# Ada rows two ahead, fetches behind the softening, and the opening's ada sums in two halves of the array

## The chip, the cores and the metric

The kernel runs on one core of a Trainium2 chip. The metric is the device time of one execution in microseconds, the median over several runs. Names of engines: PE or TensorE does matmuls (PEld is its weight load), ACT or ScalarE activations and casts, DVE or VectorE elementwise work, POOL or GpSimd small helpers, SP or SyncE issues most DMAs.

## The reference

Two layers of a diffusion transformer on 256 latent tokens `x` and 256 context tokens `ctx`, width 1024, all in fp32. Layer 0 mixes by retention, layer 1 by neighbourhood attention; each has an MLP with a hidden width of 4096.

```python
for i in range(DEPTH):
    mod = (silu_c @ ada_w[i] + ada_b[i])[:, None, :]      # ada_w[i]: 1024 x 6144
    mod_c = silu_cc @ ada_w[i] + ada_b[i]
    sh1, sc1, g1, sh2, sc2, g2 = jnp.split(mod, 6, axis=-1)
    ...
    h = x * (1.0 + sc1) + sh1
    hc = ctx * (1.0 + sc1c) + sh1c
    y, yc = retention_mixer(...) if i % 2 == 0 else neighbourhood_mixer(...)
    x = layer_norm(DN_ALPHA * x + g1 * y, ln_g[i, 0], ln_b[i, 0])
    h = x * (1.0 + sc2) + sh2
    x = layer_norm(DN_ALPHA * x + g2 * sq_relu_mlp(h, mlp_w1[i], mlp_w2[i]), ln_g[i, 1], ln_b[i, 1])
    # layer 0 does the same for ctx
```

The neighbourhood attention adds a bias to scores of 32 heads and takes a softmax over 512 local and 256 context columns. The ada products (one row per kind of token times a 1024 x 6144 matrix) give shift, scale and gate of every layer.

## The kernel before, in words

**Products.** Every fp32 product is made of three fp32r products: an operand is split into `hi` (a cast on ACT) and `lo` (a subtraction on DVE), and hi·hi, lo·hi and hi·lo are summed in PSUM. Weights come in units of 512 KB: `fetch` asks SP for a `raw` tile and casts it, `lows` subtracts, `take` hands units to the matmuls. The `raw` tiles come from a pool of four buffers, `rawp`, and the ada rows of the background (`rawa`) come from the same four. SP issues loads in the order of the program, and a load waits until its buffer is let go.

**Queues.** `pe.on`, `act.on`, `dve.on` and `sp.on` say where an engine keeps the order in which the code is written. Where they are off, a scheduler orders the instructions; in the middle of the layer-0 MLP it does.

**Background.** The ada products after the first chunks are not done on PE. `bg_stream` weighs one ada row tile per step on DVE (`weigh`, tile `acc` or `spare`), keeping one load ahead. After eight steps a part is complete; `folded` sums it into `red`, and a closure goes into `due`: `ada_columns` or `ada_gate`, a small matmul (`pada<-red,cst` in the trace) with DVE and DMA work behind it. The next call of `bg` runs what is in `due` and then the next step. In the layer-0 MLP `bg` is called once after each weight unit of the second product. A unit there is 24 matmuls: four token tiles (`mm2`), two row blocks, three products. `bg_max` is 31 before the MLP of layer 0 and 87 in it. The gate of the MLP, `G2`, is read back from DRAM (`grow`) by `load_gate`, in two broadcasts of 512 KB.

**MLP, second product.** Two halves of 512 output columns, each with four PSUM banks `p2` and eight units; after a half `accumulate` multiplies each bank by the gate on DVE (`acc<-p,G`). There are eight PSUM banks in all. The trace cuts numbers off names, so `p1` and `p2` are both `p` there.

**Opening.** Eight chunks of 128 columns of the model width. For each chunk `chunk_sums` makes the ada sums for shift and scale on PE: 16 matmuls with 32 output rows, dealt to four column groups of the array (`pada<-rawq,cT`); `chunk_row` copies the sums to SBUF; `chunk_columns` turns them into columns with two matmuls (`pada<-cst,row`), `chunk_turn` transposes the tokens (`pt<-cst,R`, `pada<-cst,R`), `chunk_modulate` makes `hTh` and `hTl`, and `chunk_q` and `part_v` project. Between them stand the parts of the chunk before.

**Attention of layer 1.** A list `STEPS` gives, for each group of heads, how many units to fetch and split before the softening (`early`), after it (`late`) and after the inversion (`last`), and which projections to run. A step sends 12 score matmuls (`pqk`), softens (four reductions on DVE, four exponentials on ACT), runs a projection, and turns the probabilities of the step before (`ppt`, copied to `pt` by ACT and DVE, `flip`).

```python
gather(n + 1); turned(n)
fetch(early); lows(early)
scores(n + 2); soften(n + 2)
fetch(late); lows(late)
run(before); flip(n + 1); invert(n + 2); fetch(last); attend(n); run(after)
lows(100 if n < len(STEPS) - 2 else len(STEPS) - 1 - n)
```

Of the kernel before, what the change touches and what calls it, by code (L numbers as in the profile page):

```python
# [17 lines left out]
P = 128  # L18
# [86 lines left out]
def kernel(  # L105
# [50 lines left out]
    def bank(s="ps"):  # L156
        return psp.tile([P, 512], F32, tag="ps", name=nm(s))
# [279 lines left out]
    def ada_columns(l, w, red, c0, nt):  # L437

        pr = bank("pada")
        for j in range(4):  # L440
            pe.matmul(
                pr[32 * j : 32 * j + 32, 0 : 8 * nt],
                lhsT=cv("fold"),
                rhs=red[:, :nt].rearrange("p t (k j) -> p j (t k)", j=4)[:, j],
                start=True,
                stop=True,
                tile_position=(0, 32 * j),
            )
        dve.tensor_add(
            out=mods[l, w][:, :, c0 : c0 + 4, :],  # L450
            in0=(
                pr[:, 0:16].rearrange("p (t s k) -> p s k t", t=2, s=2)
                if nt == 2
                else pr[:, 0:8].rearrange("p (s k) -> p s k", s=2).unsqueeze(3).broadcast_to([P, 2, 4, 2])
            ),
            in1=acol[:, COLUMNS.index((l, w)), :, c0 : c0 + 4].unsqueeze(3).broadcast_to([P, 2, 4, 2]),
        )

    def ada_gate(l, w, red, nt):

        tmp = scr("gate")[0:32, :]
        bias, tot, row = tmp[:, 0:32], tmp[:, 64 : 64 + 32 * nt], tmp[:, 128 : 128 + 32 * nt]
        g = (3 * w + 2) * D
        pool.dma_start(out=bias, in_=ada_b[l][g : g + D].rearrange("(b i) -> b i", i=32))
        pr = bank("pada")
        pe.matmul(
            pr[0:32, 0 : 32 * nt], lhsT=cv("fold"), rhs=red[:, :nt].rearrange("p t b -> p (t b)"),
            start=True, stop=True, tile_position=(0, 0),
        )
        dve.transpose(out=tot, in_=pr[0:32, 0 : 32 * nt])  # L470
        dve.tensor_add(
            out=row.rearrange("p (t i) -> p t i", t=nt), in0=tot.rearrange("p (t i) -> p t i", t=nt),
            in1=bias.unsqueeze(1).broadcast_to([32, nt, 32]),
        )
        for t in range(nt):
            pool.dma_start(
                out=grow[l, w][t].rearrange("(b i) -> b i", i=32), in_=row[:, 32 * t : 32 * t + 32]
            )
# [3 lines left out]
    def bg_load(l, w, part, offs, n):  # L482

        if (l, w, part) not in EARLY:
            return ada_load(l, n, offs)
        raw = rawp.tile([P, 2, 512], F32, tag="raw", name=nm("rawa"))
        w_ap = ada_w[l][256 * (n % 4) : 256 * (n % 4) + 256, offs[n // 4] : offs[n // 4] + 512]
        sp.dma_start(out=raw[:], in_=w_ap.rearrange("(k p) n -> p k n", p=P))
        return raw
# [8 lines left out]

    due = []

    def flush():
        while due:
            due.pop(0)()

    def bg_stream():


        plan = []
        for l, w, part in (
            list(EARLY)  # L510
            + [(0, 1, 2), (1, 0, 0), (1, 0, 1), (1, 0, 2), (1, 1, 0), (1, 1, 1), (1, 1, 2)]
        ):
            sh, sc, g = 3 * w * D, (3 * w + 1) * D, (3 * w + 2) * D
            offs = (sh + 512 * part, sc + 512 * part) if part < 2 else (g, g + 512)
            for n in range(KC):
                plan.append((l, w, part, offs, n))
        nxt = bg_load(*plan[0])
        yield
        for step, (l, w, part, offs, n) in enumerate(plan):
            raw = nxt  # L520
            if step + 1 < len(plan):
                nxt = bg_load(*plan[step + 1])

            nt = 2 if l == 0 or (w == 0 and part < 2) else 1
            if n == 0:
                red = smp.tile([P, 2, 32], F32, tag="red", name=nm("red"), bufs=2)
            if (l, w, part) in EARLY:
                dve.on = True
                for kk in range(2):
                    for t in range(nt):  # L530
                        weigh(spare(t), raw[:, kk, :], t, 2 * (n % 4) + kk, n % 4 == 0 and kk == 0)
                dve.on = False
                if n % 4 == 3:
                    yield
                    for t in range(nt):
                        folded(red, spare(t), t, 512 * (n // 4), 512)
            else:
                if n == 0:
                    acc = slot(S_VL, [P, 2, D], F32, "acc")
                for t in range(nt):  # L540

                    dve.on = n == 0 and l == 0
                    weigh(acc[:, t], raw[:].rearrange("p a n -> p (a n)"), t, n, n == 0)
                    dve.on = False
                if n == KC - 1:
                    for t in range(nt):
                        folded(red, acc[:, t], t, 0, D)
            if n == KC - 1:
                if part < 2:
                    due.append(lambda a=(l, w, red, 4 * part, nt): ada_columns(*a))  # L550
                else:
                    due.append(lambda a=(l, w, red, nt): ada_gate(*a))
            yield

    bgs = bg_stream()
# [5 lines left out]
    def bg(n=1):  # L561
        for _ in range(n):
            if bg_done[0] < bg_max[0]:
                flush()
                bg_done[0] += 1
                next(bgs, None)

# [190 lines left out]
    def chunk_loads(k):  # L758
        chunk_ada(k)
        chunk_x(k)  # L760
        ws[k] = Weights(k)
# [43 lines left out]
        dve.tensor_add(out=strip(h)[:, 1], in0=e[0], in1=dt[:, 3])  # L805
        dve.tensor_add(out=strip(h)[:, 0], in0=e[2], in1=e[3])

    prs, pts, rows = {}, {}, {}

    def chunk_sums(k, i):  # L810

        if k not in prs:
            prs[k] = bank("pada")
        for kk in range(KC):
            j = kk % 4
            pe.matmul(
                prs[k][32 * j : 32 * j + 32, tsl(i)],
                lhsT=cT[:, kk, :, :].rearrange("p a t -> p (a t)"),
                rhs=adas[k](i, kk),
                start=(kk < 4),  # L820
                stop=(kk >= 4),
                tile_position=(0, 32 * j),
            )

    def chunk_row(k, cols=slice(0, 2 * P)):
        if cols.start == 0:
# [14 lines left out]

    KINDS = slice(0, NLAT), slice(NLAT, NT)

    def chunk_turn(k):

        pts[k] = bank("pt")[:, 0:256], prs[k][:, 256:512]
        for t in range(4):
            pe.transpose(pts[k][t // 2][:, tsl(t % 2)], R[t][:, tsl(k)], ident)

    def modulated(e, out_ap, pt, k, a):  # L850
# [47 lines left out]
    turn_over(3)  # L898
    chunk_sums(0, 1)
    chunk_row(0, tsl(1))  # L900
    chunk_turn(0)
    chunk_columns(0)
    turn_over(4)
    w = ws[0]
    w.high(w.Q)
    chunk_modulate(0, lambda: (w.high(w.V), w.low(w.Q)))
# [6 lines left out]
    for k in range(KC):  # L913
        if k == 0:
            dt = slot(S_VL, [P, 4, 384], F32, "dt")
            sp.dma_start(out=dt[:, 0], in_=dist)
        if k == 3:
            sp.dma_start(out=cst1[:], in_=consts[:, NC0:])
            lrows = ln_rows()
        if k:  # L920
            chunk_q(k, ((0, 0),))
            part_v(k, 0, 0)
            chunk_q(k, ((1, 0), (0, 1)))
        if k < KC - 1:
            for i in range(2):
                chunk_sums(k + 1, i)
            chunk_turn(k + 1)
            ws[k + 1].high()
            chunk_row(k + 1)
            if k > 2:  # L930
                ws[k + 1].low()
        if k < 4:
            chunk_loads(k + 4)
        part_v(k, 1, 0)
        if k < KC - 1:
            chunk_columns(k + 1)
            chunk_modulate(k + 1, lambda: None if k > 2 else ws[k + 1].low())
        part_v(k, 0, 1)
        if k == 1:
            tabs = strip_tables(dt)  # L940
        if 1 < k < 6:
            make_strip(k - 2, *tabs)
        if k == KC - 1:
            ln_columns(lrows)
        if k > 5:
            take(0, 2 * (k - 5))
# [295 lines left out]


    HS = [S_T0, S_T1, S_SH, S_SL, S_TH, S_TL, S_GS, S_VH]
    LAT, ALL, CTX = slice(0, NLAT), slice(0, NT), slice(NLAT, NT)

    def mm1(us, sl, pb, ks=range(KC), at=0):
# [22 lines left out]
    for hf in range(2):  # L1270
# [67 lines left out]
        for half in range(2):  # L1338
# [14 lines left out]
            for u in range(8 - nheld):  # L1353
                (un,) = take(1)
                for t in range(4):
                    mm2(t, u, un)
                bg()
                if G2 is None and u == 3:
                    G2 = load_gate(0, 1)
            if not last:  # L1360
                for t in range(4):
                    accumulate(pb[t], t, half, G2)
# [421 lines left out]
    def K(g):  # L1784
        return lambda: k_part(g)
# [7 lines left out]
    def W(half, t):  # L1793
# [7 lines left out]
    REST = lambda: rest_evac(rest_mm(1))  # L1801
    STEPS = [
        (1, 0, 0, [K(2)], []),
        (2, 0, 0, [K(3)], []),
        (2, 0, 0, [K(4)], []),
        (1, 0, 0, [K(5)], []),
        (2, 0, 0, [Q(2)], []),
        (1, 1, 0, [V(0)], []),
        (0, 0, 0, [V(1)], []),
        (0, 0, 0, [V(2)], [REST]),  # L1810
        (0, 0, 0, [V(3)], []),
# [399 lines left out]
```

## Time and profile before

| | |
|---|---|
| median of 3 runs | 1186.33 us (1186.08 to 1186.82) |
| the profiled execution | 1185.37 us |
| its span, first to last instruction | 1183.3 us |
| mean granted TensorE clock | 0.997 |
| PE / PEld busy | 1170.2 us (99%) / 988.2 us (84%) |
| DVE / ACT / POOL busy | 841.4 (71%) / 480.0 (41%) / 212.6 us (18%) |
| DMA | 195.10 MB, mean 165 GB/s |

Busy time counts matmuls whose ends are modelled, so an engine that is busy 99% of the span can still have matmuls that start later than they could. Such losses are read from the starts in the timeline, and from the number of matmuls in stretches of equal length. The span is 2.07 us shorter than the execution's time.

### The profile page before, as it was taken

The numbers are of one execution on the slowest core, as the hardware profiler recorded it, in microseconds if no ns is written. First come the engines' busy times: TensorE is split into PE (matmuls) and PEld (weight loads), VectorE is DVE, ScalarE is ACT, GpSimd is POOL, SyncE is SP. The second block draws the span as 40 slices with busy tenths as digits, with TensorE's granted clock in tenths as the row PEclk, the third lists the DMA queues.
The fourth block names the chain that finished last, engine by engine and source line by source line (L and its number), as shares of the span: only waits on it lengthen the run. The fifth ranks groups of instructions, "written<-read, shape, count | busy, mean of one in ns | idle before, by whom it ended". The sixth has DMA issues, their size and how long they took to land.

```text
span 1183.3 us, 17724 instructions
## 1 busy us (share of the span) xinstructions
PE 1170.2 (99%) x6822; PEld 988.2 (84%) x6822; DVE 841.4 (71%) x1331; ACT 480.0 (41%) x819; POOL 212.6 (18%) x364
## 2 busy tenths in 40 slices
PE   9999999999999999999899999999999999999997
PEld 7788888888888889888788888889878878999886
DVE  3877684876798586897867775668566689877446
ACT  3643332232323255442122333137466666756341
POOL 0102001100200340870203000223344430000001
PEclk9999999999999999999999999999999999999999
DMA  9932551543364226776566665646244334666660
GB/s 277 273 125 92 157 165 48 179 143 107 124 194 146 89 67 222 211 186 227 174 196 202 212 213 189 199 138 203 84 140 125 107 116 160 217 208 200 231 211 37
DMA packets 139091, 195.10 MB, mean 165 GB/s; under 512 B 9936, under 2 KB 81136, under 8 KB 139008
## 3 DMA queue, kind: packets, MB, share of 16 engines
q1 hardware_dynamic: 130880, 182.03, 48.5%
q0 software_dynamic: 6976, 9.39, 3.5%
q10 hardware_dynamic: 1152, 2.56, 0.6%
q8 instruction: 53, 0.87, 0.3%
q14 instruction: 30, 0.25, 0.1%
HBM read 189.12 MB, written 5.75 MB: 165 GB/s over the span
## 4 chain that ended last, share of the span: by engine, by line
PE 85%; DVE 5%; DMA 5%; issue 2%; ACT 2%; POOL 0%; SPq 0%; DVEq 0%; ACTq 0%; POOLq 0%
PE p L84 34%; PE pq L84 8%; PE pv L84 7%; PE pw L84 7%; PE pg L84 7%; PE pn L84 5%; PE pnv L84 4%; PE po L84 3%; DMA rawa<-in_ada_w_dram 2%; DVE acc L84 2%; DMA raw<-in_mlp_w_dram 2%; PE pnw L84 1%; PE pS L84 1%; DVE lo L84 1%; PE ppt L84 1%
## 5 line engine op out<-in xcount | busy, mean ns | idle before, releaser
L84 ACT CAST hi<-raw 128x1024 fp32r<-128x1024 f32 (+2 forms) x228 | 232.1, 1034 | 318.7 <-DMA raw<-in_mlp_w_dram 82.9
L84 DVE TENSOR_TENSOR lo<-raw,hi 128x1024 fp32r<-128x1024 f32 (+2 forms) x228 | 275.0, 1220 | 99.2 <-ACT hi L84 99.1
L84 PE MATMUL p<-hi,hid 128*128 128x512 f32 (+1 forms) x832 | 243.2, 375 | 0.0
L84 PEld LDWEIGHTS p<-hi,hid 128*128 128x128 f32 x832 | 153.0, 189 | 28.2
L84 PE MATMUL p<-hTh,lo 128*128 128x256 f32 (+1 forms) x512 | 165.8, 326 | 0.0
L84 PE MATMUL p<-hTl,hi 128*128 128x256 f32 (+1 forms) x512 | 165.8, 326 | 0.0
L84 PE MATMUL p<-hTh,hi 128*128 128x256 f32 (+1 forms) x512 | 162.9, 328 | 0.0
L84 PE MATMUL p<-lo,hid 128*128 128x512 f32 (+1 forms) x416 | 156.0, 375 | 0.0
L84 DVE SCALAR_TENSOR_TENSOR acc<-rawa,scol,acc 128x1024 f32<-128x1024 f32 x70 | 91.9, 1322 | 66.5 <-DMA rawa<-in_ada_w_dram 66.5
L84 PEld LDWEIGHTS p<-hTh,lo 128*128 128x128 f32 x512 | 96.4, 188 | 8.8
L84 PEld LDWEIGHTS p<-hTl,hi 128*128 128x128 f32 x512 | 96.4, 188 | 8.6
L84 PEld LDWEIGHTS p<-hTh,hi 128*128 128x128 f32 x512 | 94.2, 188 | 8.7
L84 PEld LDWEIGHTS p<-lo,hid 128*128 128x128 f32 x416 | 78.7, 189 | 13.7
L84 ACT CAST hid<-r 128x256 fp32r<-128x256 f32 (+1 forms) x64 | 32.0, 502 | 115.3 <-DVE r L84 115.1
L84 POOL TENSOR_TENSOR rstd<-rstd,misc 128x1 f32<-128x1 f32 x28 | 19.2, 687 | 214.1 <-DVE rstd L84 212.9
L84 DVE SCALAR_TENSOR_TENSOR strips<-rawa,scol,strips 128x512 f32<-128x512 f32 x84 | 57.6, 747 | 0.0
L84 ACT ACTIVATE s<-s,mn 128x512 f32<-128x512 f32 x64 | 45.5, 714 | 26.2 <-DVE mn L84 26.2
L84 POOL TENSOR_SCALAR rstd<-mv 128x1 f32<-128x1 f32 x16 | 3.9, 244 | 290.0 <-DVE mv L84 290.0
L84 POOL TENSOR_TENSOR R<-R,acc 128x512 f32<-128x512 f32 x16 | 24.8, 1566 | 165.9 <-DVE acc L84 165.8
L84 PE MATMUL pw<-hi,oh 128*128 128x512 f32 x128 | 50.9, 398 | 0.0
L84 PE MATMUL pg<-hi,hTh 128*128 128x512 f32 x128 | 50.6, 395 | 0.0
L84 PE MATMUL pw<-hi,ol 128*128 128x512 f32 x128 | 49.9, 390 | 0.0
(236 smaller groups left out, 2328.2 us busy)
## 6 DMA issues: line engine op xcount, KB each, us to landing
raw<-in_mlp_w_dram SPq DMA_DIRECT2D x128, 512.0 KB, 4.5
rawa<-in_ada_w_dram SPq DMA_DIRECT2D x80, 512.0 KB, 3.9
raw<-in_ret_w_in_dram SPq DMA_DIRECT2D x42, 512.0 KB, 3.6
raw<-in_nat_w_in_dram SPq DMA_DIRECT2D x24, 512.0 KB, 4.5
rawq<-in_ada_w_dram SPq DMA_DIRECT2D x16, 512.0 KB, 6.1
raw<-in_ret_w_o_dram SPq DMA_DIRECT2D x16, 512.0 KB, 3.6
bias<-rpb_rows POOLq DMA_DIRECT2D x32, 128.0 KB, 2.9
raw<-in_nat_w_o_dram SPq DMA_DIRECT2D x8, 512.0 KB, 3.7
```

The lines of the kernel that those rows point to most:

```text
L84: r = f(*args, **kwargs)
```

## The change

It has several parts that touch different stages:

- `bg_stream` keeps two ada rows loaded ahead from step 24 on, in place of one.
- What is in `due` is tagged with the step that put it there. Where `bg_max` is 31 the next call of `bg` runs it, as before; where it is 87, the call after that.
- In the opening, for chunks 1 to 7, the sums are dealt so that shift goes to the two lower column groups and scale to the two upper ones, each over 128 columns. The copy to SBUF has 128 columns in place of 256. Two matmuls of 64 rows, at row 0 and row 64 of the array, turn them into columns in two banks, and two additions on DVE replace one.
- Chunk 0 turns the latent tokens, makes its columns, and then turns the context tokens. In chunks 1 to 3 the product of `hTl` with `hi` for q stands behind the sums and loads of the next chunk.
- The gate `G2` is loaded in four pieces after units 3, 4, 6 and 7.
- In `STEPS` the fetches of the first steps move from `early` to `late`.

```diff
-    def flush():
-        while due:
-            due.pop(0)()
+    def flush(before=1 << 30):
+        while due and due[0][0] < before:
+            due.pop(0)[1]()
...
-        nxt = bg_load(*plan[0])
+        loaded = [bg_load(*plan[0])]
...
-            raw = nxt
-            if step + 1 < len(plan):
-                nxt = bg_load(*plan[step + 1])
+            raw = loaded.pop(0)
+            ahead = 1 if step < len(EARLY) * KC else 2
+            while len(loaded) < min(ahead, len(plan) - 1 - step):
+                loaded.append(bg_load(*plan[step + 1 + len(loaded)]))
...
-                    due.append(lambda a=(l, w, red, 4 * part, nt): ada_columns(*a))
+                    due.append((bg_done[0], lambda a=(l, w, red, 4 * part, nt): ada_columns(*a)))
...
-                flush()
+                flush(bg_done[0] + (bg_max[0] == 31))
...
+    def chunk_pairs(k):
+        prs[k] = bank("pada")
+        for kk in range(KC):
+            for i in range(2):
+                j = 2 * i + kk % 2
+                pe.matmul(
+                    prs[k][32 * j : 32 * j + 32, :P],
...
+                    tile_position=(0, 32 * j),
+                )
+
+    def chunk_columns_of_pairs(k):
+        outs = prs[k][:, 0:2], ptb[k][:, 256:258]
+        for i in range(2):
+            js = slice(64 * i, 64 * i + 64)
+            pe.matmul(
+                outs[i], lhsT=rows[k][js, :P], rhs=cv("sel4")[js, 0:2], start=True, stop=True,
+                tile_position=(64 * i, 0),
+            )
+        for i in range(2):
+            dve.tensor_scalar_add(out=mods[0, 0][:, i, k, :], in0=outs[i], scalar1=bcol[:, i, k : k + 1])
...
-    chunk_turn(0)
+    chunk_turn(0, (0, 1))
     chunk_columns(0)
-    turn_over(4)
+    chunk_turn(0, (2, 3))
+    turn_over(3)
...
-            chunk_q(k, ((1, 0), (0, 1)))
+            chunk_q(k, ((1, 0),))
+        late = 0 < k < 4
+        if k and not late:
+            chunk_q(k, ((0, 1),))
         if k < KC - 1:
-            for i in range(2):
-                chunk_sums(k + 1, i)
+            chunk_pairs(k + 1)
             chunk_turn(k + 1)
             ws[k + 1].high()
-            chunk_row(k + 1)
+            chunk_row(k + 1, slice(0, P))
...
+        if late:
+            chunk_q(k, ((0, 1),))
         part_v(k, 1, 0)
         if k < KC - 1:
-            chunk_columns(k + 1)
+            chunk_columns_of_pairs(k + 1)
...
-                if G2 is None and u == 3:
-                    G2 = load_gate(0, 1)
+                if hf == 0 and half == 0 and u > 2:
+                    if G2 is None:
+                        G2 = cpool.tile([P, 2, D], F32, tag="G", name=nm("G"))
+                    if u != 5:
+                        t, sl = u % 2 if u < 5 else u - 6, HALF[u > 5]
+                        act.dma_start(out=G2[:, t, sl], in_=grow[0, 1][t : t + 1, sl].broadcast_to([P, 512]))
...
     STEPS = [
         (1, 0, 0, [K(2)], []),
-        (2, 0, 0, [K(3)], []),
-        (2, 0, 0, [K(4)], []),
-        (1, 0, 0, [K(5)], []),
-        (2, 0, 0, [Q(2)], []),
-        (1, 1, 0, [V(0)], []),
+        (0, 2, 0, [K(3)], []),
+        (0, 2, 0, [K(4)], []),
+        (0, 1, 0, [K(5)], []),
+        (0, 2, 1, [Q(2)], []),
+        (0, 1, 0, [V(0)], []),
```

The built order of PE in the MLP of layer 0, second half of the outputs (first pass): the ada columns `pada` between two weight units. Before, they stand between the first and second unit of the half (`hi_753`, `hi_757`):

```order
L84 MATMUL p2_775_4972<-lo_754_4822,hid_614_3766 128x512
L84 MATMUL p2_775_4972<-hi_753_4821,hid_614_3766 128x512
L84 MATMUL pada_779_5003<-red_737_4710,cst1_82 32x16 [waits DVE_49]
L84 MATMUL pada_779_5003<-red_737_4710,cst1_82 32x16 x3
L84 MATMUL p2_772_4969<-hi_757_4855,hid_615_3767 128x512 [waits Activation_49]
L84 MATMUL p2_772_4969<-lo_758_4856,hid_615_3767 128x512
```

After, between the second and third unit (`hi_759`, `hi_763`):

```order
L84 MATMUL p2_777_4983<-lo_760_4865,hid_616_3774 128x512
L84 MATMUL p2_777_4983<-hi_759_4864,hid_616_3774 128x512
L84 MATMUL pada_787_5050<-red_737_4711,cst1_82 32x16 [waits DVE_49]
L84 MATMUL pada_787_5050<-red_737_4711,cst1_82 32x16 x3
L84 MATMUL p2_774_4980<-hi_763_4898,hid_643_4094 128x512 [waits Activation_49]
L84 MATMUL p2_774_4980<-lo_764_4899,hid_643_4094 128x512
```

The columns moved by one unit of 24 matmuls, and still wait for DVE.

The built order of ACT around the gate `G` in the first half of the same product. Before, one broadcast stands on each side of a cast:

```order
L84 CAST hi_4716<-raw_4714 128x1024
L576 DMA G_4816<-grow_111 128x1024
L84 CAST hi_4750<-raw_4748 128x1024
L576 DMA G_4816<-grow_111 128x1024
L84 CAST hi_4784<-raw_4782 128x1024
```

After:

```order
L84 CAST hi_4717<-raw_4715 128x1024
L84 CAST hi_4759<-raw_4757 128x1024
L84 DMA G_4825<-grow_111 128x512 x2
L84 CAST hi_4793<-raw_4791 128x1024
L84 DMA G_4825<-grow_111 128x512 x2
L84 CAST hi_4829<-raw_4827 128x1024
```

The loads moved behind one more cast, and the four pieces stand in two pairs on the two sides of the cast after it.

The built order of DVE in the second changed step of `STEPS` (`lo` is the split of a fetched unit, `s<-pqk,bias` a reduction, `kT` the split of the projection that runs in the step). Before:

```order
L84 TENSOR_TENSOR oTl_6928<-rt_7294,oTh_6927 128x4x32
L84 TENSOR_TENSOR lo_7423<-raw_7420,hi_7422 128x1024
L84 TENSOR_TENSOR lo_7428<-raw_7425,hi_7427 128x1024
L84 ISA s_7450,mn_7448<-pqk_7432,bias_6842 128x512
L84 ISA mn_7448 128x1
L84 ISA s_7453,mn_7448<-pqk_7433,bias_6842 128x512
```

After:

```order
L84 TENSOR_TENSOR oTl_6937<-rt_7303,oTh_6936 128x4x32
L84 ISA s_7447,mn_7445<-pqk_7429,bias_6851 128x512
L84 ISA mn_7445 128x1
L84 ISA s_7450,mn_7445<-pqk_7430,bias_6851 128x512
L84 ISA mn_7445 128x1
L84 ISA s_7453,mn_7445<-pqk_7431,bias_6851 128x512
L84 ISA mn_7445 128x1
L84 ISA s_7456,mn_7445<-pqk_7432,bias_6851 128x512
L84 ISA mn_7445 128x1
L84 TENSOR_TENSOR lo_7462<-raw_7459,hi_7461 128x1024
L84 TENSOR_TENSOR lo_7467<-raw_7464,hi_7466 128x1024
L84 TENSOR_TENSOR kT_7471<-pn_7472,kT_7471 128x512
```

The two splits moved from ahead of the four reductions to behind them, next to the split of `kT`.

More of the change, by code (lines that the diff above doesn't have):

```diff
@@ L549, in bg_stream @@
                 if part < 2:
-                    due.append(lambda a=(l, w, red, 4 * part, nt): ada_columns(*a))
+                    due.append((bg_done[0], lambda a=(l, w, red, 4 * part, nt): ada_columns(*a)))
                 else:
-                    due.append(lambda a=(l, w, red, nt): ada_gate(*a))
+                    due.append((bg_done[0], lambda a=(l, w, red, nt): ada_gate(*a)))
             yield
@@ L806, in make_strip @@
         dve.tensor_add(out=strip(h)[:, 0], in0=e[2], in1=e[3])
-    prs, pts, rows = {}, {}, {}
+    prs, pts, ptb, rows = {}, {}, {}, {}
     def chunk_sums(k, i):
@@ L823, in chunk_sums @@
             )
+    def chunk_pairs(k):
[5 more added lines that the diff above has]
+                    prs[k][32 * j : 32 * j + 32, :P],
+                    lhsT=cT[:, kk, :, :].rearrange("p a t -> p (a t)"),
+                    rhs=adas[k](i, kk),
+                    start=(kk < 2),
+                    stop=(kk >= KC - 2),
+                    tile_position=(0, 32 * j),
[10 more added lines that the diff above has]
+            dve.tensor_scalar_add(out=mods[0, 0][:, i, k, :], in0=outs[i], scalar1=bcol[:, i, k : k + 1])
     def chunk_row(k, cols=slice(0, 2 * P)):
@@ L842, with chunk_turn @@
     KINDS = slice(0, NLAT), slice(NLAT, NT)
-    def chunk_turn(k):
-        pts[k] = bank("pt")[:, 0:256], prs[k][:, 256:512]
-        for t in range(4):
+    def chunk_turn(k, ts=range(4)):
+        if k not in pts:
+            ptb[k] = bank("pt")
+            pts[k] = ptb[k][:, 0:256], (prs[k][:, 256:512] if k else bank("pt")[:, 0:256])
+        for t in ts:
             pe.transpose(pts[k][t // 2][:, tsl(t % 2)], R[t][:, tsl(k)], ident)
@@ L1244 @@
     HS = [S_T0, S_T1, S_SH, S_SL, S_TH, S_TL, S_GS, S_VH]
+    HALF = slice(0, 512), slice(512, 1024)
     LAT, ALL, CTX = slice(0, NLAT), slice(0, NT), slice(NLAT, NT)
```

## The prediction

> **What bounds the kernel now.** I read the page first, for the share of each engine and the chain that ended last.
>
> ```profile
> PE 1170.2 (99%) x6822; PEld 988.2 (84%) x6822; DVE 841.4 (71%) x1331; ACT 480.0 (41%) x819; POOL 212.6 (18%) x364
> ...
> PE 85%; DVE 5%; DMA 5%; issue 2%; ACT 2%; POOL 0%; SPq 0%; DVEq 0%; ACTq 0%; POOLq 0%
> ```
>
> TensorE is busy for 1170.2 of 1183.3 us, and the change removes no matmul of size. So it can gain only where TensorE stands still, or where its instructions stretch. I looked for those places in the table by stretches of 20 us, where a full stretch of the MLP holds 90 matmuls.
>
> ```profile
> 540.00:560.00 20.00, 20.00 (x90) 16.57 (x89) 12.56 (x11) 4.24 (x4) 0.00 (x0) 1.00 0.70 243
> 560.00:580.00 20.00, 16.82 (x81) 13.62 (x80) 14.19 (x15) 4.21 (x4) 1.15 (x1) 0.98 0.53 164
> 580.00:600.00 20.00, 20.00 (x83) 16.35 (x83) 15.43 (x13) 3.17 (x3) 5.83 (x4) 0.93 0.55 180
> 600.00:620.00 20.00, 20.00 (x90) 16.54 (x89) 15.02 (x13) 3.35 (x4) 0.00 (x0) 1.00 0.60 191
> ```
>
> The columns after the length are PE, PEld, DVE, ACT and POOL busy, then the granted clock, the DMA share and GB/s. One stretch has 16.82 us of PE, and the next has 83 matmuls at a clock of 0.93. TensorE's timeline there (start, length, tile; idle time and releaser in brackets):
>
> ```profile
> 575.26 0.39 PE L84 MATMUL p<-hi,hid 128*128 128x512 f32 x1
> 578.82 0.26 PE L84 MATMUL pada<-red,cst 128*32 128x16 f32 x8 [3.18 <-DVE acc L84]
> 579.01 0.53 PE L84 MATMUL p<-hi,hid 128*128 128x512 f32 x1
> 579.35 0.62 PE L84 MATMUL p<-lo,hid 128*128 128x512 f32 x1
> ```
>
> How fast it goes undisturbed, the first and last of the 24 matmuls of an earlier weight unit show:
>
> ```profile
> 526.07 0.39 PE L84 MATMUL p<-hi,hid 128*128 128x512 f32 x1
> ...
> 531.28 0.39 PE L84 MATMUL p<-hi,hid 128*128 128x512 f32 x1
> ```
>
> 23 steps in 5.21 us are 0.227 us a matmul, 5.44 us a unit. The ada matmul should have begun at 575.49 and began at 578.82: 3.3 us lost. In the stretch from 580 there are 7 matmuls fewer than 90, 7 x 0.227 = 1.6 us. Together 4.9 us, the largest loss that I found. What it waited for is on VectorE, whose queue is filled from SyncE's loads:
>
> ```profile
> 575.75 1.28 DVE L84 SCALAR_TENSOR_TENSOR acc<-rawa,scol,acc 128x1024 f32<-128x1024 f32 x1 [3.33 <-DMA rawa<-in_ada_w_dram]
> 576.95 1.22 DVE L84 TENSOR_TENSOR lo<-raw,hi 128x1024 fp32r<-128x1024 f32 x1
> 578.08 1.28 DVE L84 TENSOR_TENSOR acc<-p,G 128x512 f32<-128x512 f32 x2
> ```
>
> ```profile
> 545.42 0.37 SPq L84 DMA_DIRECT2D rawa<-in_ada_w_dram  x1
> ...
> 571.12 0.37 SPq L84 DMA_DIRECT2D rawa<-in_ada_w_dram  x1
> ...
> 578.19 0.37 SPq L84 DMA_DIRECT2D rawa<-in_ada_w_dram  x1
> ```
>
> The ada columns need a PSUM bank. It is freed by the first "acc<-p,G" of the half before, which stands in VectorE's queue behind a weighing that waited 3.33 us for its ada row, and behind a lo. From 545.42 to 578.19 five rows went out, 6.55 us a row, against the 5.44 us that TensorE needs for a weight unit. The row and weight loads share a ring of four buffers, so this loop is slower than TensorE for a while and lives on weights split ahead.
>
> **Part 1, the ada matmuls one background step later.** The order shows the columns after the second unit of the half in place of the first, and they wait for the same kind of event, the first gated sum of the half before. TensorE reaches them at 575.49 + 5.44 = 580.93. If VectorE keeps its times, the bank is free at 578.08 + 0.64 = 578.72, half of the pair's 1.28 us: 2.2 us to spare. The built order has the ring of loads in the same step with the weights (the row weighed last before the sum is let go by the lo of the third unit in both), so I expect no other time for it. Gain: 4.9 us, bounds 0 and 4.9. What is late next is nothing I can see: the other ada matmuls do not wait today, and only get a step more. The matmul itself, and the one that builds the gate, come 5.44 us later, so ScalarE gets its gate loads later too.
>
> **Part 2, rows two ahead and the gate in four pieces.** No load, weighing or byte more. With a ring of four, a row asked for earlier still waits for the same lo, so I take 0 for the steady loop. The four gate pieces of 256 KB stand together in ScalarE's built order, two before and two after one cast, so they are not spread over units as their text says. ScalarE waits there for the gate's write, with the casts of the next weights behind it; it waits there today as well, and the stretch from 540 to 560 has its 90 matmuls. I take 0, with 1 us either way.
>
> **Part 3, the fetches behind the softening.** In the second layer each step sends 12 score matmuls, which need four PSUM banks that the step's transposes leave. ScalarE, VectorE and TensorE in the second of the five changed steps:
>
> ```profile
> 868.64 2.00 ACT L84 CAST hi<-raw 128x1024 fp32r<-128x1024 f32 x2
> ...
> 872.73 0.73 ACT L84 ACTIVATE s<-s,mn 128x512 f32<-128x512 f32 x1 [2.08 <-DVE mn L84]
> ...
> 875.57 0.57 ACT L84 CAST kT<-pn 128x512 fp32r<-128x512 f32 x1
> 876.03 0.85 ACT L84 COPY pt<-ppt 128x384 f32<-128x384 f32 x2
> ```
>
> ```profile
> 868.61 0.29 DVE L84 TENSOR_TENSOR oTl<-rt,oTh 128x128 fp32r<-128x128 f32 x1 [0.37 <-ACT oTh L84]
> 869.72 2.36 DVE L84 TENSOR_TENSOR lo<-raw,hi 128x1024 fp32r<-128x1024 f32 x2 [0.82 <-ACT hi L84]
> 872.00 0.68 DVE L84 CUSTOM_DVE_ANT_1 s<-pqk,bias 128x512 f32<-128x512 f32 x1
> ...
> 876.17 0.69 DVE L84 TENSOR_TENSOR kT<-pn,kT 128x512 fp32r<-128x512 f32 x1 [1.64 <-ACT kT L84]
> 876.77 1.15 DVE L84 COPY pt<-ppt 128x384 f32<-128x384 f32 x2
> ```
>
> ```profile
> 866.46 1.12 PE L84 MATMUL pqk<-kT,qT 32*128 32x512 f32 x12
> 867.51 0.50 PE L84 MATMUL pn<-hTh,hi 128*128 128x512 f32 x1
> ...
> 875.74 0.50 PE L84 MATMUL pqk<-kT,qT 32*128 32x512 f32 x2
> 876.56 1.31 PE L84 MATMUL pqk<-kT,qT 32*128 32x512 f32 x10 [0.32 <-ACT pt L84]
> 877.80 0.50 PE L84 MATMUL pn<-hTh,hi 128*128 128x512 f32 x1
> ```
>
> From the first score to the next projection the first block takes 867.51 - 866.46 = 1.05 us, the second 877.80 - 875.74 = 2.06, so 1.0 us more for the copies out of the banks. After the change the four reductions can start at 868.9 (oTl done) in place of 872.00, and the exponentials with them; then come the casts (2.00) and the lows (2.36). Replayed: four reductions of 0.68 to 871.6, four exponentials of 0.73 from 869.6 to 872.5, casts to 874.5, the second lo from 874.7 to 875.9, then the kT subtraction (0.69) and VectorE's copies from 876.6 in place of 876.77; ScalarE's copies from 875.1 in place of 876.03. The engines do the same work, and only the waits of each for the other (0.82 and 2.08 us in the brackets) go. So 0.2 to 0.9 us in this step, less in those of one fetch. I take 1.1 us over the five. Bounds: at best each step loses what the second does, 5 x 1.0 = 5.0; at worst one lo (1.18, half of 2.36) is late in each of the two-fetch steps, 3 x 1.2 = 3.5 us more time. The fetch also issues its load on SyncE's queue, where in this stage only such loads stand:
>
> ```profile
> raw<-in_nat_w_in_dram SPq DMA_DIRECT2D x24, 512.0 KB, 4.5
> ```
>
> A second lo that ends at 875.9 in place of 872.0 lets the load of the fourth unit after it go 3.9 us later; that unit is cast two steps of 875.74 - 866.46 = 9.3 us on, and its load takes 4.5, so it is still there in time.
>
> **Part 4, the opening.** TensorE's rows of one chunk and of another, its weight loads among them:
>
> ```profile
> 9.02 0.20 PEld L84 LDWEIGHTS pada<-cst,R 128*128 128x128 f32 x2 [0.29 <-DVE row L84]
> ```
>
> ```profile
> 27.41 0.20 PEld L84 LDWEIGHTS pt<-cst,R 128*128 128x128 f32 x2 [0.20 <-issue]
> ...
> 29.38 0.16 DVE L84 TENSOR_TENSOR mod<-pada,bcol 128x4 f32<-128x4 f32 x1 [0.84 <-PE pada L84]
> ...
> 30.24 0.30 PEld L84 LDWEIGHTS pq<-hTh,hi 128*128 128x128 f32 x2 [0.29 <-ACT hTh L84]
> ...
> 32.29 0.30 PEld L84 LDWEIGHTS pq<-hTl,hi 128*128 128x128 f32 x2 [0.38 <-DVE hTl L84]
> ```
>
> ```profile
> 48.05 0.50 PE L84 MATMUL pada<-cst,row 128*128 128x2 f32 x4
> 48.41 1.19 PE L84 MATMUL pv<-lo,hTh 128*128 128x512 f32 x4
> ```
>
> Moving the hTl products behind the sums covers the wait of 0.38 in three chunks; about 0.2 of it reaches TensorE, as its matmuls run behind its loads: 3 x 0.2 = 0.6 us gained. Chunk 0 sends its columns ahead of two transposes that waited for the row: 0.2. The row copy halves, but the columns stand behind four other matmuls, so that is hidden. The columns take 48.41 - 48.05 = 0.36 us in four passes; side by side two passes' time, 0.18 less. A second addition on VectorE (0.16) then stands ahead of hTh, for which TensorE already waits (0.29): the two cancel. Left is the price of another tile shape. The loads after the 32-column sums wait 0.20 us for nothing but issue. Two such steps, in and out of the half-array shape, would be 0.4 a chunk and 2.8 us in seven chunks, none would be 0; I take 0.1 a chunk, 0.7 us, since the row is of a step between full and quarter columns and this one keeps all columns. The Trainium skill, TensorEngine Tiling (Array Packing), Key Properties, speaks against the edit: a change of the tiling mode, not of the tile alone, drains the array; by it all seven chunks would pay in full, and the opening would lose 2.0 us. Opening: 0.6 + 0.2 - 0.7 = 0.1 gained, bounds 2.1 gained (0.8 and 7 x 0.18) and 2.0 lost (2.8 less 0.8).
>
> **Sum.** The profiled execution took 1185.37 us, 0.96 under the median of 1186.33. 4.9 + 0 + 1.1 + 0.1 = 6.1 us off: 1179.3 for such an execution, 1180.2 for the median.
>
> **Rivals.**
>
> The bank comes a loop later. Then the columns wait again: 578.72 + 6.55 = 585.3 against 580.9 is a stall of 4.4 us, and part 1 gains about nothing: 1186.3 - 1.2 = 1185.1. For it speaks that one more ada row is weighed ahead of the sum in the built order; against it, that this row is let go by the same unit's lo. Chance 0.14.
>
> The rows held ahead starve the weights: slower. Two of four buffers hold rows, the weights come one by one, and TensorE falls to the loop's 6.55 us a unit once its reserve is used. Eight units at 6.55 - 5.44 = 1.1 are 8.9 us: 1180.2 + 8.9 = 1189.1. It decides where a lo ends after TensorE has finished the unit before. The rows issued at 545 to 578 show that such a loop exists; against it, the stretches before and after hold 90 matmuls despite it. Chance 0.10.
>
> The softening and the opening go against me while the first part holds: 4.9 - 3.5 - 2.0 = 0.6 better at worst, 1185.7, and about 1184 where half of that comes true. Chance 0.11.
>
> The gains are larger: a softening near its bound of 5 us, or an opening near 2: 1176. Chance 0.07. The forecast keeps 0.58.
>
> **How the numbers follow.** The likeliest case gives 1180.2. Its own range is 1177.5 to 1183. The first and third rivals end at 1184 to 1186, so the range reaches to 1186.5, and below to 1176.3, which leaves out the slow rival and the tail of the large gains. A difference of 0.2% (2.4 us) is about what a measurement of this kernel can tell from none. Faster: the forecast, the large gains and some of the mixed case and a little of the first rival, 0.75; same 0.14; slower 0.11.
>
> **What would show it.** Right: no wait on "acc" ahead of "pada<-red,cst" near 580 us, 90 matmuls in the stretches there and a clock of 1.00; the score blocks at 867 to 907 us under 1.7 us; chunks of the opening within 0.2 us of today's. Wrong: a bracket of several us on pada or on "p<-hi,hid", a lo that TensorE waits for between 540 and 780 us, pt copies later than now, or a chunk that is 0.4 us longer.

## The result, and the profile after

The changed kernel takes 1193.76 us (median of 7 runs, 1189.14 to 1195.0), the kernel before 1186.82 (1184.93 to 1188.14). The ratio is 1.0047 (95% interval 1.0031 to 1.0063). Forecast were 1180.2 us and a range of 1176.3 to 1186.5: the change is slower where faster was expected. Run again beside other kernels it gave 1.0062 (1.0043 to 1.0080).

The first answer is TensorE's table of waits, what it waited for, in all, times and longest. After:

```profile
PE p L84 <- DVE lo L84: 7.0, 6, 2.8
PE p L84 <- ACT hi L84: 1.9, 3, 1.0
...
PE pada L84 <- DVE acc L84: 0.2, 1, 0.2
```

The wait of 3.2 us ahead of the ada columns is gone, as forecast; 0.2 us is left of it. In its place TensorE waits nine times, 8.9 us, for weights that are not yet cast or split. The same stretches of 20 us as before:

```profile
560.00:580.00 20.00, 20.00 (x90) 16.57 (x89) 15.60 (x15) 4.21 (x4) 0.00 (x0) 1.00 0.70 229
580.00:600.00 20.00, 19.82 (x95) 16.09 (x94) 17.17 (x16) 3.19 (x4) 7.00 (x4) 1.00 0.50 159
...
620.00:640.00 20.00, 17.18 (x82) 13.65 (x81) 12.03 (x11) 1.54 (x2) 6.99 (x4) 1.00 0.63 197
```

The loss of 560 to 600 has moved to 620 and later, into the second pass of the layer-0 MLP. (The MLP runs in two passes, each with a first and a second product over half of the hidden width.) TensorE's timeline has the ada columns, the pass's first matmul and the first long wait; the last line here is the pass's first matmul in the kernel before:

```profile
581.82 0.26 PE L84 MATMUL pada<-red,cst 128*32 128x16 f32 x8 [0.18 <-DVE acc L84]
...
614.80 0.39 PE L84 MATMUL p<-hTh,hi 128*128 128x512 f32 x1
```

```profile
632.25 0.50 PE L84 MATMUL p<-hTh,lo 128*128 128x512 f32 x1 [2.82 <-DVE lo L84]
```

```profile
618.85 0.39 PE L84 MATMUL p<-hTh,hi 128*128 128x512 f32 x1
```

The second pass begins at 614.80 in place of 618.85, so 4.1 us of part 1 were in hand there. The wait at 632.25 takes most of it, and the others after it the rest and more.

The times of the stages tell where the whole went. Each is the time in us from the start of a stage's first matmul to the start of its last, read from the trace of one profiled execution; for the opening it is the start of the last matmul of its sums, here and wherever the end of the sums is given. The attention is taken from its first to its last score matmul.

| kernel | end of the opening's sums | layer-0 MLP | its first pass | its second pass | attention | last MLP |
|---|---|---|---|---|---|---|
| before | 52.8 | 360.6 | 182.8 | 177.7 | 153.0 | 165.2 |
| after | 53.2 | 368.3 | 178.2 | 190.1 | 150.8 | 168.2 |
| after, once more | 53.7 | 367.5 | 178.2 | 189.2 | 150.8 | 165.4 |

The layer-0 MLP is 7 to 8 us longer, the attention 2.2 us shorter, the opening up to 0.9 longer. The first pass did gain 4.6 us, near the 4.9 of part 1, and the second lost 12.4. The nine waits are 8.9 us of that; the rest is in the starts around them, which come later than the brackets say (at 632.25 the start is 3.21 us after the one before it and the next is 0.34 behind, where 0.227 is usual). What happened at 620 is seen on VectorE. Before:

```profile
617.93 1.22 DVE L84 TENSOR_TENSOR lo<-raw,hi 128x1024 fp32r<-128x1024 f32 x1
622.82 2.60 DVE L84 SCALAR_TENSOR_TENSOR acc<-rawa,scol,acc 128x1024 f32<-128x1024 f32 x2 [3.67 <-DMA rawa<-in_ada_w_dram]
625.34 1.22 DVE L84 TENSOR_TENSOR lo<-raw,hi 128x1024 fp32r<-128x1024 f32 x1
626.47 2.48 DVE L84 TENSOR_TENSOR acc<-p,G 128x512 f32<-128x512 f32 x4
```

After:

```profile
622.42 1.28 DVE L84 SCALAR_TENSOR_TENSOR acc<-rawa,scol,acc 128x1024 f32<-128x1024 f32 x1 [4.49 <-DMA rawa<-in_ada_w_dram]
623.63 1.22 DVE L84 TENSOR_TENSOR lo<-raw,hi 128x1024 fp32r<-128x1024 f32 x1
627.24 1.28 DVE L84 SCALAR_TENSOR_TENSOR acc<-rawa,scol,acc 128x1024 f32<-128x1024 f32 x1 [2.39 <-DMA rawa<-in_ada_w_dram]
629.77 1.28 DVE L84 SCALAR_TENSOR_TENSOR acc<-rawa,scol,acc 128x1024 f32<-128x1024 f32 x1 [1.25 <-DMA rawa<-in_ada_w_dram]
630.98 1.22 DVE L84 TENSOR_TENSOR lo<-raw,hi 128x1024 fp32r<-128x1024 f32 x1
632.11 2.48 DVE L84 TENSOR_TENSOR acc<-p,G 128x512 f32<-128x512 f32 x4
```

The gated sums of the half stand at 632.11 in place of 626.47, although TensorE has left the first pass 4.1 us earlier. Ahead of them stand three weighings that each wait for a row (4.49, 2.39 and 1.25 us), in place of two with one wait (3.67), and the lo that ends at 632.2 is the one TensorE waits for at 632.25. The built orders say the same: ahead of the first gated sum of the first pass VectorE has split 95 units in either kernel, and weighed 35 times before, 37 times after (two weighings are one row there).

### The profile page after: what moved, and what is told of

Its sections match the earlier page's. It is cut to its first block, busy times and chain, and to the rows that moved or that the text cites. A ratio compares the mean times of both kernels' runs of the same rounds, so it can differ in the third digit from the quotient of the medians.

```text
span 1192.8 us, 17728 instructions
## 1 busy us (share of the span) xinstructions
PE 1173.8 (98%) x6821; PEld 986.8 (83%) x6821; DVE 842.0 (71%) x1338; ACT 480.0 (40%) x819; POOL 212.2 (18%) x364
## 4 chain that ended last, share of the span: by engine, by line
PE 74%; DMA 12%; DVE 8%; issue 3%; ACT 2%; POOL 0%; SPq 0%; DVEq 0%; ACTq 0%; POOLq 0%
PE p L84 22%; PE pq L84 8%; DMA rawa<-in_ada_w_dram 7%; PE pv L84 7%; PE pw L84 7%; PE pg L84 7%; PE pn L84 5%; PE pnv L84 4%; DVE acc L84 4%; DMA raw<-in_mlp_w_dram 3%; PE po L84 3%; DVE lo L84 2%; PE ppt L84 2%; PE pnw L84 1%; PE pS L84 1%
```

## The experiments

Ratios are to the kernel before, in runs beside it, with 95% intervals. One caution: the layer-0 MLP of kernels that have the same code there took 360.6 us (before), 361.5 (fetches alone), 366.6 (opening alone) and 358.4 (moves alone) in their profiles. The second pass alone took 177.7, 180.8, 186.1 and 179.5 of it. So one profile of that stage says little, and the ratios decide.

**One row ahead, all else as changed.**

```diff
-            ahead = 1 if step < len(EARLY) * KC else 2
+            ahead = 1
```

> The changed kernel with one ada row ahead throughout, all else as changed. Ring theory (the second row ahead puts each weighing a place ahead of the splits of the weights, so the second pass of the layer-0 MLP starts without reserve): the waits of PE on lo and hi between 630 and 732 us, 10.4 us in the profile after, go, and the wait before pada near 580 stays away; 1193.8 - 10.4 = about 1183 us, or a little under. Rival (the later gate, its four pieces and the deferred ada matmuls delay VectorE's loop): the waits stay, 1190 us or more.

Measured: 1186.87 us, ratio 1.0019 (1.0006 to 1.0032). Waits on lo:

```profile
PE p L84 <- DVE lo L84: 2.8, 3, 1.8
```

The second row costs most of the loss. But neither forecast came true: the waits shrink and do not go (the table above has 8.9 us of them for the 10.4 of the expectation), and what is left is no gain, but 0.2% slower than before.

**The second row alone, on the kernel before.** The diff is that of `bg_stream` in the change.

> The kernel before with only the second ada row ahead. Ring theory: PE waits on lo and hi in the second pass of the MLP, 7 to 10 us, and the wait before pada near 579 is still there or longer: 1192 to 1200 us. Rival: no such waits, 1186 to 1188 us, as before.

Measured: 1189.69 us, ratio 1.0044 (1.0027 to 1.0061): as much as the whole change loses, and less than the 1192 to 1200 that was expected. Nor did it come where it was expected. The table of waits:

```profile
PE pada L84 <- DVE acc L84: 2.7, 1, 2.7
PE pada L84 <- DVE red L84: 2.5, 1, 2.5
...
PE p L84 <- DVE lo L84: 0.5, 1, 0.5
```

With the ada matmuls at their old place TensorE waits there, twice (at 534 and 582 us), and hardly for lo. Its layer-0 MLP is 366.0 us, and here the first pass pays: 187.6 us in place of 182.8, the second 178.5. The loss is about the same whichever instruction waits.

**The deferral alone.** The diff is that of `flush` and `due`.

> The kernel before with only the ada matmuls one background step later. Ring theory, and the prediction's first part: the wait of 3.2 us before pada and the slow clock behind it go, nothing new comes, 1186.8 - 4.9 = about 1182 us. Rival (the deferral itself delays the gate and VectorE's loop): waits on lo in 630 to 730 us, 1187 to 1192 us.

Measured: 1187.25 us, ratio 1.0018 (1.0000 to 1.0035), no gain. The wait on acc is gone from the table, and this is in its place:

```profile
PE p L84 <- DVE lo L84: 3.0, 3, 1.8
...
PE p L84 <- ACT hi L84: 0.6, 1, 0.6
```

3.6 us in place of 3.2. The first pass takes 178.0 us, 4.9 less than before and just what part 1 forecast; the second takes 184.2, 6.5 more. The stall ahead of the ada columns may have given VectorE's loop time to get ahead of TensorE, which without it meets the loop 60 to 110 us later (640 to 688 us). That is a reading of one profile: the opening alone, which keeps the stall (2.4 us), waited 5.0 us for lo in its second pass all the same. The ratio alone shows that the gain does not last.

**The fetches behind the softening, alone.** The diff is that of `STEPS`.

> The kernel before with only the fetches moved behind the softening. The prediction's third part: 1.1 us less (1185.7), with the score blocks at 867 to 907 us shorter. Rival (copies out of the banks come later): 0 to 3.5 us more, 1187 to 1190 us.

Measured: 1184.94 us, ratio 0.9991 (0.9972 to 1.0010). The attention takes 151.1 us in place of 153.0. The gain is seen in every profile with this edit (150.8 to 151.3 in eight, 152.7 to 153.0 in the six without), though the whole kernel's interval holds 1. In the changed kernel's timeline the two steps of the score blocks that the prediction looked at, with the projection that follows, read:

```profile
874.78 0.97 PE L84 MATMUL pqk<-kT,qT 32*128 32x512 f32 x12
875.68 0.50 PE L84 MATMUL pn<-hTh,hi 128*128 128x512 f32 x1
...
883.90 0.97 PE L84 MATMUL pqk<-kT,qT 32*128 32x512 f32 x12
884.80 0.50 PE L84 MATMUL pn<-hTh,hi 128*128 128x512 f32 x1
```

0.90 us from scores to projection in both, as against 1.05 and 2.06 before.

**The changed kernel once more.**

> The changed kernel once more, unchanged, to see what of its time is the kernel's and what an execution's. Its profile after has two things that its parts do not: 10 us of waits in the layer-0 MLP, and 256-column matmuls of the last MLP at 117.7 ns in place of 113.3 (3.0 us in all). If both belong to the kernel, both are there again; if the second is an execution's, it goes and comes, and the median lies at 1190 to 1194.

Measured: 1194.25 us, ratio 1.0062 (1.0043 to 1.0080). The waits on lo are there again (6.1 us, five times); the slower 256-column matmuls of the last MLP are not. The first belongs to the kernel, the second to an execution. The 3.0 us of the expectation are 2.8 by the table of stages (168.2 and 165.4).

**Two rows ahead only until step 50.**

```diff
-            ahead = 1 if step < len(EARLY) * KC else 2
+            ahead = 2 if len(EARLY) * KC <= step < 50 else 1
```

> The changed kernel with two rows ahead only from step 24 to 50, one from there on, so that the second pass of the layer-0 MLP has the order of one row ahead. Order theory (what costs is one weighing more in front of the weights' splits): the cost comes back when the row is given back, PE's waits on lo after 630 us shrink to the 3 to 5 us of the kernel with one row ahead, about 1187 us. Rival (the cost is the buffer held in the first pass): 1190 us or more.

Measured: 1188.1 us, ratio 1.0017 (1.0005 to 1.0030), its interval below that of the changed kernel beside it. The first pass had its two rows; when the second row is given back before the second pass, nearly all of its cost goes. So, with the ada columns a step later, the cost isn't paid where the row is taken, but later, where by our reading the loop has no reserve left.

**No row ahead, on the kernel before.** From step 24 on the row is asked for in the step that weighs it.

```diff
-            raw = nxt
-            if step + 1 < len(plan):
-                nxt = bg_load(*plan[step + 1])
+            if step > len(EARLY) * KC:
+                nxt = bg_load(*plan[step])
+            raw = nxt
+            if step < len(EARLY) * KC:
+                nxt = bg_load(*plan[step + 1])
```

> The kernel before with no ada row held ahead from step 24 on: the row is asked for in the step that weighs it. Order theory: the weights stand one weighing further ahead, so PE's waits in the layer-0 MLP (3.3 us before pada, none on lo) shrink: 1182 to 1185 us. Rival (a row must be asked for early or VectorE waits a whole transfer, 3.9 us, for each): the loop is longer, 1190 us or more.

Measured: 1185.88 us, ratio 0.9988 (0.9974 to 1.0001), on the edge of what can be told, and just above the 1182 to 1185 that was expected. The rival fell: no loop is longer. The wait on acc is gone without any deferral, the layer-0 MLP takes 358.0 us, and ahead of the first gated sum there are 33 weighings, one row fewer. What is left of that stage's waits:

```profile
PE pada L84 <- DVE red L84: 1.0, 1, 1.0
PE p L84 <- DVE lo L84: 0.8, 1, 0.8
```

**The opening alone.** The diff is all of the change's opening.

> The kernel before with only the changed opening. By the prediction 0.1 us less, bounds 2.1 less and 2.0 more. By the profile after, whose last opening sums end at 53.21 us against 52.77 before, 0.4 to 0.6 us more: the 64-row columns cost more in chunks 4 to 7 than the moved products gain in 1 to 3.

Measured: 1186.72 us, ratio 1.0003 (0.9988 to 1.0018), nothing that can be told in the whole. Its sums end at 53.69 us. Over all profiles whose opening ran at full speed, they end at 53.1 to 54.0 with the whole changed opening (five) and 52.6 to 52.9 without (six). The profile of the columns after and before:

```profile
28.99 0.27 PE L84 MATMUL pada<-cst,row 64*128 64x2 f32 x1
29.00 0.27 PE L84 MATMUL pt<-cst,row 64*128 64x2 f32 x1
29.12 0.25 PE L84 MATMUL pada<-cst,row 64*128 64x2 f32 x1
29.13 0.25 PE L84 MATMUL pt<-cst,row 64*128 64x2 f32 x1
29.31 1.20 PE L84 MATMUL pv<-lo,hTh 128*128 128x512 f32 x4
30.49 0.70 PE L84 MATMUL pq<-hTh,hi 128*128 128x512 f32 x2
```

```profile
28.84 0.50 PE L84 MATMUL pada<-cst,row 128*128 128x2 f32 x4
29.20 1.19 PE L84 MATMUL pv<-lo,hTh 128*128 128x512 f32 x4
30.27 0.69 PE L84 MATMUL pq<-hTh,hi 128*128 128x512 f32 x2
```

The two halves do run side by side (their starts are 0.01 us apart), yet the four passes take 29.31 - 28.99 = 0.32 us as against 0.36, and the next chunk's first product comes 1.18 us after them as against 1.07: the second addition stands ahead of the `hTh` that it needs. The loads of the first of these column matmuls, after and before, show a third difference:

```profile
28.99 0.18 PEld L84 LDWEIGHTS pada<-cst,row 64*128 64x128 f32 x1 [0.36 <-issue]
```

```profile
28.61 0.65 PEld L84 LDWEIGHTS pada<-cst,row 128*128 128x128 f32 x4
```

The half-array load waits 0.36 us for nothing but issue, and the full one does not wait. In the starts of the matmuls 0.10 us of that is left: the columns come 0.33 us after the product ahead of them, where they came 0.23 us after it. So a chunk has 0.10 - 0.04 + 0.11 = 0.17 us more, near the 0.14 by which the last chunks lengthened (6.48 us in place of 6.34).

**The opening's moves alone,** with the old sums and columns.

> The kernel before with the opening's moved products and the split turn of chunk 0, but the sums and columns as before. By the prediction's terms 0.8 us less than before, so that the last opening sums end near 52.0 us (52.77 before, 53.2 to 53.5 with the whole change). If the moves gain nothing, they end at 52.8, and the whole opening's loss is not the columns'.

Measured: 1186.02 us, ratio 1.0015 (1.0000 to 1.0029), no gain. Its profile is of an execution whose opening ran slow (below), so the end of the sums can't be compared; the last experiment has the same opening and ends them at 52.54, 0.2 us ahead of before and just outside the 52.6 to 52.9 of the kernels without the moves. In that experiment's timeline the steps from one chunk's sums to the next are 6.43, 6.34 and 6.80 us where they were 6.54, 6.56 and 6.32: what the moved products gain in the earlier ones comes back in the one where they meet those that were never moved.

**No row ahead in the changed kernel.**

> The changed kernel with no ada row held ahead from step 24 on, all else as changed. Order theory: the waits on lo between 630 and 710 us shrink below the 5 us that the changed kernel with one row ahead has, and its layer-0 MLP, 368 us with two rows and 361.3 with one, comes near the 358.0 of the kernel before with none: 1184 to 1186 us. Rival (the deferral and the gate's pieces have a cost of their own in that stage): 361 us or more, 1187 or more.

Measured: 1186.62 us, ratio 1.0019 (1.0004 to 1.0033). The layer-0 MLP of its profile is 359.5 us, but by the ratio it is no better than the changed kernel with one row, and slower than before: neither forecast's time came. So once the second row is gone, something else of the change costs about 0.2%; the deferral alone measured as much (1.0018), and with the changed opening the sums end 0.3 to 1.3 us later in the profiles. The gate's four pieces were not tried alone.

**No row ahead, and the fetches behind the softening.** This takes from the change what gains, and turns round what costs.

> The kernel before with no row ahead and the fetches behind the softening: the layer-0 MLP of 358.0 us and an attention of 151.0 us in place of 360.6 and 153.0, so 4 us less than before in a profile like those, 0.2 to 0.35% faster.

Measured: 1182.16 us, ratio 0.9982 (0.9966 to 0.9997): faster than the kernel before by a narrow margin, a little less than the 0.2 to 0.35% that was expected, and so faster than the changed kernel too. The layer-0 MLP takes 358.2 us and the attention 151.2 in its profile.

**The same with the opening's moves.**

> The same with the opening's moves too: 0.8 us less again if the moves gain what the prediction said, no difference that can be measured if they don't.

Measured: 1182.63 us, ratio 0.9988 (0.9973 to 1.0003), no difference that can be told from the one without.

## Why the prediction was wrong

**The step that failed** is in part 2: "a row asked for earlier still waits for the same lo, so I take 0 for the steady loop". The ring of loads is the same, but the order in it is not: the built order has one row's weighings more in front of the same splits (37 in place of 35). The term was put at nothing and measured 0.44% alone, about 5.2 us, and most of it went when the row was taken away or given back. The size is near the 6.55 us that a row takes of the loop, so our reading is that TensorE then lacks one row's time; no run shows that link itself. In the changed kernel the first pass hid the loss and the second, where SyncE's loads go out as two units and two or three rows in turn, paid 12.4 us; in the run of the second row alone, with the ada columns at their old place, the first pass paid. A lo that TensorE waits for between 540 and 780 us stood among the prediction's own signs of being wrong, and it came.

**The second rival** had the mechanism, at a chance of 0.10: TensorE in want of weights. Its price, 8.9 us more in that stage than forecast, was too small: the stage grew by 7 to 8 us where 4.9 less was forecast, so it is 12 to 13 us above the forecast. And its eight units are priced by the first pass's loop (545 to 578 us), while the changed kernel lost in the second pass. Against it stood "the stretches before and after hold 90 matmuls despite it". That was a wrong reading: a stretch without a wait shows that the reserve was not used up, not how much of it there was.

**Part 1** failed in another way. The wait went, as worked out (0.2 us left, and 95 starts in the stretch from 580 with the eight of the ada columns), and the first pass got its 4.9 us in the deferral alone, 4.6 in the changed kernel; but the kernel did not. "What is late next is nothing I can see" was the fault: the weights were late next. Alone the deferral gave 1.0018. We read this so that VectorE's loop of rows and splits bounds the middle of this MLP, and a wait of TensorE is only the place where the two meet; the medians fit that, and do not show it.

**The first rival**, a bank that comes a loop later, came by half. Part 1 assumed that "VectorE keeps its times", with the first gated sum at 578.08; in the changed kernel it starts at

```profile
581.08 1.28 DVE L84 TENSOR_TENSOR acc<-p,G 128x512 f32<-128x512 f32 x2
```

3.0 us later, not 6.55. That used up the 2.2 us that were to spare and left the wait of 0.2 us. With the deferral alone it starts at 577.01 and nothing waits for it; with the second row alone at 581.40, so it is the row that puts it off.

**Part 3** had the right mechanism, and a size too small: 1.1 us forecast, 1.9 to 2.2 measured in the attention of the profiles. The replay of the step came out within 0.3 us: 7.9 us later than in it, ScalarE's copies start at 882.76 (875.1 in the replay) and VectorE's at 884.35 (876.6). But it gave the step 0.2 to 0.9 us, and the block lost 1.16 (2.06 to 0.90); and another 0.6 went in a later block, which took 1.54 us at 905.57 before and 0.91 at 912.43 after. A small part is that the replay set the four reductions 0.68 us apart, their length; they start 0.62 apart:

```profile
866.80 0.69 DVE L84 CUSTOM_DVE_ANT_1 s<-pqk,bias 128x512 f32<-128x512 f32 x1
...
867.42 0.69 DVE L84 CUSTOM_DVE_ANT_1 s<-pqk,bias 128x512 f32<-128x512 f32 x1
```

**Part 4** came out within its bounds: 0.1 us gained was forecast, 0.4 to 0.9 lost in two profiles of the changed kernel. The moves were taken at 0.8 and bring 0.2 at most, since what the earlier chunks gain, the fourth step gives back. The price of a chunk was near, 0.1 us forecast and 0.14 measured, but not its terms: of the 0.18 us that two passes fewer in a row should save, 0.04 are left, and 0.10 is lost ahead of them. The Trainium skill's rule (TensorEngine Tiling (Array Packing), Key Properties), that a change of the mode drains the array, agrees in sign with these rows: 0.14 us a chunk against the 0.4 of the full price.

**A sum** of the third rival is wrong: 4.9 - 3.5 - 2.0 is 0.6 us worse than before, not better, so that rival reached to 1186.9, beyond the range. It did not come, since the softening gained.

**What stays open.** In one ring that one queue fills in order, the row's buffer and the place of its weighing move together, and no run parts them. That the deferral itself costs is at the edge of its interval, and the gate's four pieces, which part 2 put at nothing within 1 us, have no run of their own.

## What to carry to other kernels

When a helper loop on another engine feeds the bound engine, find its time per step and the reserve in hand before removing a wait: the wait may be the loop's chance to catch up, and can come back at the next thing the loop makes. Loading further ahead in a ring shared with the critical stream is not free, since it puts work that can wait in front of work that can't. Where it was one row too many, the opposite edit, asking later, is the next thing to try.

## What the runs showed of the hardware

The opening does not always start at full speed. TensorE in the stretches from 6 to 12 and 12 to 18 us of the kernel before, and of the changed kernel with one row ahead:

```profile
6.00:12.00 6.00, 5.39 (x56) 3.93 (x56) 2.71 (x9) 1.95 (x4) 0.00 (x0) 1.00 1.07 291
12.00:18.00 6.00, 6.00 (x58) 4.46 (x57) 3.01 (x7) 1.96 (x3) 0.00 (x0) 1.00 1.18 308
```

```profile
6.00:12.00 6.00, 6.00 (x48) 4.40 (x48) 1.14 (x6) 0.89 (x3) 0.00 (x0) 1.00 1.17 302
12.00:18.00 6.00, 5.91 (x37) 4.19 (x39) 2.47 (x5) 1.89 (x4) 0.00 (x0) 1.00 1.19 306
```

In the second, matmuls of 512 columns start 0.43 us apart until 17.6 us, in place of 0.227, and the opening's sums end at 57.03 us. The view prints a granted clock of 1.00 for both, but it counts time without a record as full, and the trace's record of the clock begins only at 17.63 us in this execution, as against 5.90 in the kernel before. Behind the wait at 579 us of the kernel before, where the record says 0.50, matmuls start 0.43 us apart too; so our reading is that the opening ran at half the clock until 17.63 us. Two of the fourteen profiled executions show it (the record begins at 4.0 to 6.9 us in the other twelve). Both have the changed chunk 0, which eight of the fourteen have; whether it comes with it, two can't tell.

The half clock does not follow every long wait. The record has 0.50 for 3.4 us or more behind waits of TensorE of 1.78, 2.51, 2.52, 2.66, 2.96 and 3.18 us in the layer-0 MLP, and none behind waits of 1.85, 2.00, 2.40, 2.43, 2.71 and 2.82 us there. So the 1.6 us that part 1 put on the slow clock belong to some executions and not to all.

In one execution of the changed kernel the 256-column matmuls of the last MLP ran at 117.7 ns for all of its first product, in another at 113.3, about as in every other kernel; that is the 2.8 us between 168.2 and 165.4 in the table of stages. The two executions:

```profile
1050.00:1070.00 20.00, 20.00 (x172) 20.00 (x171) 14.36 (x21) 12.60 (x22) 0.00 (x0) 1.00 0.65 199
```

```profile
1050.00:1070.00 20.00, 20.00 (x179) 20.00 (x178) 14.60 (x22) 12.22 (x23) 0.00 (x0) 1.00 0.63 197
```

172 starts in 20 us as against 179, at a granted clock of 1.00. No run tells its cause.
